# A trunk's squared-ReLU MLPs: two of the weight combinations of the seven-product scheme formed by adding DMAs, the down products reordered, one operand buffer moved

## The chip, the cores and the metric

The kernel runs on one core of a Trainium2 chip. The core has TensorE (PE) for matrix products, VectorE (DVE) and ScalarE (ACT) for elementwise work, GpSimd (POOL) and SyncE (SP), which here issues nearly all transfers. Each engine works off its own queue in program order and waits on semaphores for the others. The time is the device time of the one core, in microseconds (us).

## The reference, cut to what matters

Four layers, each a mixer (latent attention or gated linear attention) and then an MLP with a squared ReLU. There are two MLPs (here MLP 0 and MLP 1) with weights of their own, 512 tokens, D = 1024 and a hidden width of 4096:

```python
def rms_norm(x, gain):
    xf = x.astype(jnp.float32)
    y = xf * lax.rsqrt(jnp.mean(xf * xf, axis=-1, keepdims=True) + EPS)
    return (y * gain.astype(jnp.float32)).astype(x.dtype)

def sq_relu_mlp(xn, w_up, w_down):
    hid = jnp.square(jax.nn.relu(xn @ w_up))
    return hid @ w_down

x = x + mix.astype(x.dtype)
x = x + sq_relu_mlp(rms_norm(x, norm_mlp[i]), w_up, w_down)
```

All data is float32. The change touches the two MLPs alone.

## The kernel before

**Numbers in two parts.** A float32 operand is split into a high and a low part (`split`, line 108): ScalarE writes the high part `wh` (line 112), VectorE the rest `wl` (line 115). A product is three matmuls, high by high, high by low and low by high. `piece` (line 145) splits 128 x 1024 values of weights; three pairs of `wh` and `wl` exist.

**Seven products in place of eight.** The MLP's products are done in the scheme of Strassen and Winograd: tokens, the contracted dimension and the output are each halved, and of a weight block's quarters 11, 12, 21 and 22 and sums of them come seven products. In `up_block` (line 838 on) a block is 512 of the 4096 hidden columns; its quarters of 512 KB are called `a11`, `a12`, `a21` and `a22`, each in a tile `raw` (128 x 1024 values) out of five buffers. The steps are s1 (11), s2 (12), s5 (the sum `s`), s6 (`s` less `a11`), s3 (`a12` less that), s7 (`a11` less `a21`) and s4 (22). The sums of weights are formed by VectorE: line 904 `s = a21 + a22`, line 919 `s - a11`, line 925 `a12 - s`, line 932 `a11 - a21`. The activations stand in tiles x0 to x7 and in the combinations T1 to T4, made once for each MLP by `combine`; a tile T0 to T3 of the profile holds one 128 rows of all four. Line 818 is the matmul of both directions. A product of a block is one piece, 24 matmuls of 128 x 256.

**Outputs.** Products that share a part of their sum go on in one PSUM bank; `seed` copies a bank. s3 and s7 add a stored product to the bank (lines 928 and 935), `finish` scales by the norm's reciprocal root and cuts at zero (line 862) and ScalarE squares (line 863). In s7 the bank read by line 935 is the one to which s4 (T4) adds next, so s4 of the same block waits for that read.

**Order.** Blocks 0 and 1 run first (their first steps while the mixer still ends), one after the other; their second halves, `a21` and `a22`, come by two transfers of 1 MB in the buffers of the down weights (line 1116). From block 2 on, the down products of the pair before are put between the steps of the up blocks. `down_block` (line 944 on) takes two blocks of hidden columns: quarters of 1 MB in three buffers (line 950), seven products of two pieces each. There VectorE forms `S = 21 + 22` (line 987), `S - 11` (line 992), `11 - 21` (line 1004) and `12 - S` (line 1019). The moving operand is the split hidden tile `h` in two buffers, h0 and h1, used in turn (`operand`). The steps of the order within an engine come from a scheduler that sets each engine's queue.

**Loads.** All weights come by SP, line 852 for the up quarters and 950 for the down quarters. A load waits until the tile's buffer has been read by its former users, and in SP's queue for the loads ahead of it. POOL issues only two small loads, at the start of the kernel.

**Pads.** `PADS` holds bytes that are left free at the start of pools, to place the operands' addresses mod 512; `hidden` is that between h1 and h0 for MLP 0 and MLP 1.

Of the kernel before, what the change touches and what calls it, by code (L numbers as in the profile page):

```python
# [49 lines left out]
def trunk_kernel(ctx: ExitStack, tc: tile.TileContext, t_in: dict, out: bass.AP, out_row: bass.AP):  # L50
# [40 lines left out]
    PADS = dict(stage=224, right=64, up=320, masks=256, keep=128, hidden=(0, 0), down_w=(224, 224))  # L91
# [9 lines left out]
    pad(opened("edge", "right"), PADS["right"])  # L101
# [164 lines left out]
    class QuadNorm(Norm):  # L266
# [25 lines left out]
        def combine(self, k, t):  # L292
            g1, g2 = (gcol(self.g, self.g0 + j) for j in (k, k + KH))
            u, v = xT[k], xT[k + KH]
            t1, t2, t3, t4 = (t[:, i] for i in range(4))
            ACT.activation(t3, u[:, second], AF.Copy, scale=g1)
            DVE.scalar_tensor_tensor(t3, v[:, second], g2, t3, ALU.mult, ALU.subtract)
            DVE.scalar_tensor_tensor(t2, u[:, first], g1, t3, ALU.mult, ALU.add)
            DVE.scalar_tensor_tensor(t4, v[:, first], g2, t2, ALU.mult, ALU.subtract)
            DVE.scalar_tensor_tensor(t1, v[:, second], g2, t2, ALU.mult, ALU.subtract)  # L300
            return t

        def difference(self, k):
            DVE.tensor_tensor(xT[k][:, second], xT[k][:, second], xT[k + KH][:, second], ALU.subtract)
# [481 lines left out]
    def out_proj(w2d, X, nxt, after, begun=None):  # L786
        for c in range(4):
# [14 lines left out]
            if c < 3:  # L802
                nxt.pair(c)
                nxt.difference(c)


    def mlp(layer, nrm, nxt, final=False):
# [5 lines left out]
        def wide_raw():  # L813
            return pool_of("down_w").tile([P, 4, 512], F32, tag="raw", bufs=3, name=uname("raw"))
# [21 lines left out]
        Q, wide, turn = {}, {}, [0, 1]  # L836

        def up_block(b):
# [20 lines left out]
            def finish(c, half, tk):  # L859
                qs = q[tk is second][:, 2 * half : 2 * half + 2]  # L860
                r = nrm.rstd[:, tk].unsqueeze(1).to_broadcast([P, 2, TH])
                DVE.scalar_tensor_tensor(qs, c, 0.0, r, ALU.max, ALU.mult)  # L862
# [37 lines left out]
            def s5():  # L900
                s = v["s"] = up.tile([P, KH, 256], F32, tag="raw", bufs=5, name=uname("raw"))
                if "a12" not in v:
                    v["a12"] = unit(0, 1)
                DVE.tensor_tensor(s, v["a21"], v["a22"], ALU.add)  # L904
# [11 lines left out]
            def s6():  # L916
                if b == 1:
                    seed(v["p1"])
                DVE.tensor_tensor(v["s"], v["s"], v["a11"], ALU.subtract)
# [4 lines left out]
            def s3():  # L924
                DVE.tensor_tensor(v["a12"], v["a12"], v["s"], ALU.subtract)  # L925
# [5 lines left out]
            def s7():  # L931
                DVE.tensor_tensor(v["a21"], v["a11"], v["a21"], ALU.subtract)  # L932
# [11 lines left out]
        def down_block(s):  # L944
            last = s == NB // 2 - 2

            def quarter(dh, fh):
# [13 lines left out]
            def product(n, a, t, evac=None):  # L961
# [23 lines left out]
            def p5():
                v["21"], v["S"] = quarter(1, 0), quarter(1, 1)
                DVE.tensor_tensor(v["S"], v["21"], v["S"], ALU.add)
# [15 lines left out]
            def p7():  # L1003
                DVE.tensor_tensor(v["21"], v["11"], v["21"], ALU.subtract)
# [709 lines left out]
```

## Time and profile before

| | us |
|---|---|
| three runs | 1081.42, 1083.45, 1085.34 (median 1083.45) |
| the profiled execution's own time | 1080.79 |
| its span in the trace | 1079.1 |
| MLP 0, from the first block's T products to the last product | about 204 to 446 |
| MLP 1, the same | about 757 to 1002 |

The span runs from the first to the last instruction of the trace; the difference to the execution's own time (1.7 us) lies around it. The page's lines give busy time by engine and by group of instructions, the views of waits what released an engine that stood idle, and the windows the busy time of each engine in a stretch. A matmul's end is modelled, so the distance of two starts tells more of its price than its own duration (0.28 us for 128 x 256, started some 0.115 us apart).

### The profile page before, as it was taken

How to read it: one execution, taken by the hardware profiler on the slowest of the kernel's cores; microseconds unless marked ns; L12 is line 12 of the kernel's file. 1: busy time of each engine (PE TensorE's matmuls, PEld its weight loads, DVE VectorE, ACT ScalarE, POOL GpSimd, SP SyncE). 2: the span in 40 equal slices, each digit the busy share in tenths (PEclk: the TensorE clock that was granted, in tenths of full speed). 3: DMA queues.
4: the chain of work that ended last, by engine and by line, in shares of the span. 5: the costliest groups of instructions: out<-in, count | busy, mean ns of one | idle time of the engine just before them, and what ended most of it. 6: DMA issues, size and time to landing. Idle time of an engine off the chain costs nothing.

```text
span 1079.1 us, 17824 instructions
## 1 busy us (share of the span) xinstructions
PE 1058.9 (98%) x7322; PEld 977.1 (91%) x7322; DVE 890.0 (82%) x1210; ACT 640.2 (59%) x934; POOL 44.5 (4%) x78
## 2 busy tenths in 40 slices
PE   9999999989999999999999999999899999999997
PEld 7788888989999999988788888888899999999986
DVE  6789879999899899967565655678999899899865
ACT  6577655566667776644334735655565667766734
POOL 6400000000000000030000000000000000000000
PEclk9999999999999999999999999999999999999999
DMA  7312017143433433260222222234324423522412
GB/s 211 95 49 79 13 31 229 42 136 99 157 98 99 157 100 96 86 203 24 62 67 78 79 79 57 61 98 138 117 79 129 146 82 134 176 76 82 137 39 79
DMA packets 97969, 107.88 MB, mean 100 GB/s; under 512 B 8048, under 2 KB 72832, under 8 KB 97888
## 3 DMA queue, kind: packets, MB, share of 16 engines
q1 hardware_dynamic: 95872, 105.52, 31.1%
q8 instruction: 57, 0.93, 0.4%
q10 hardware_dynamic: 1952, 1.21, 0.4%
q0 software_dynamic: 64, 0.02, 0.1%
q14 instruction: 24, 0.20, 0.1%
HBM read 104.64 MB, written 2.10 MB: 99 GB/s over the span
## 4 chain that ended last, share of the span: by engine, by line
PE 84%; DVE 11%; issue 2%; ACT 2%; DMA 1%; SPq 0%; DVEq 0%; ACTq 0%
PE ps L818 39%; PE ps L120 12%; PE ps L122 12%; PE ps L121 12%; DVE wl L115 4%; PE ps L137 2%; PE ps L1371 2%; DMA wraw_ckv<-in_mla_w_in_dram 1%; DVE q L862 1%; DVE h L115 1%; DVE raw L925 1%; ACT wh L112 1%; DVE raw L932 1%; DVE raw L904 0%; PE ps L1408 0%
## 5 line engine op out<-in xcount | busy, mean ns | idle before, releaser
L112 ACT ACTIVATE wh<-raw 128x1024 fp32r<-128x1024 f32 x208 | 218.9, 1057 | 155.2 <-PE ps L818 84.3
L115 DVE TENSOR_TENSOR wl<-raw,wh 128x1024 fp32r<-128x1024 f32 x208 | 251.8, 1218 | 16.6 <-ACT wh L112 16.3
L818 PE MATMUL ps<-h,wh 128*128 128x256 f32 x1344 | 170.6, 279 | 0.0
L818 PEld LDWEIGHTS ps<-h,wh 128*128 128x128 f32 x1344 | 163.0, 188 | 0.0
L818 PE MATMUL ps<-h,wl 128*128 128x256 f32 x672 | 92.3, 279 | 2.1 <-DVE wl L115 2.1
L120 PE MATMUL ps<-set,wh 128*128 128x512 f32 x232 | 92.0, 397 | 0.7 <-ACT set L245 0.7
L121 PE MATMUL ps<-set,wh 128*128 128x512 f32 x232 | 91.2, 393 | 0.6 <-DVE set L246 0.6
L122 PE MATMUL ps<-set,wl 128*128 128x512 f32 x232 | 91.1, 393 | 0.0
L112 ACT ACTIVATE wh<-wraw 128x1024 fp32r<-128x1024 f32 x41 | 43.0, 1056 | 74.0 <-PE ps L122 41.5
L818 PEld LDWEIGHTS ps<-h,wl 128*128 128x128 f32 x672 | 84.5, 188 | 2.5 <-DVE wl L115 2.5
L863 ACT ACTIVATE q<-q 128x512 f32<-128x512 f32 x64 | 40.0, 629 | 46.4 <-DVE q L862 46.2
L120 PE MATMUL ps<-wh,set 128*128 128x512 f32 x144 | 59.7, 414 | 0.0
L115 DVE TENSOR_TENSOR wl<-wraw,wh 128x1024 fp32r<-128x1024 f32 x41 | 50.3, 1230 | 10.7 <-ACT wh L112 10.6
L115 DVE TENSOR_TENSOR h<-q,h 128x1024 fp32r<-128x1024 f32 x44 | 53.6, 1220 | 4.9 <-ACT h L112 4.9
L122 PE MATMUL ps<-wh,set 128*128 128x512 f32 x144 | 56.3, 391 | 0.0
L121 PE MATMUL ps<-wl,set 128*128 128x512 f32 x144 | 56.3, 391 | 0.0
L121 PEld LDWEIGHTS ps<-set,wh 128*128 128x128 f32 x232 | 44.0, 190 | 10.5 <-DVE set L246 1.3
L120 PEld LDWEIGHTS ps<-set,wh 128*128 128x128 f32 x232 | 43.9, 190 | 10.0 <-ACT set L245 1.0
L122 PEld LDWEIGHTS ps<-set,wl 128*128 128x128 f32 x232 | 44.0, 190 | 9.0
L112 ACT ACTIVATE h<-q 128x1024 fp32r<-128x1024 f32 x44 | 46.2, 1052 | 4.8 <-DVE q L988 2.1
L818 PE MATMUL ps<-T0h,wh 128*128 128x256 f32 x128 | 33.2, 283 | 7.1 <-DVE q L935 6.7
L120 PE MATMUL ps<-hh,wh 128*128 128x512 f32 x96 | 37.4, 389 | 0.0
(512 smaller groups left out, 2778.2 us busy)
## 6 DMA issues: line engine op xcount, KB each, us to landing
raw<-in_mlp_w_down_dram SPq DMA_DIRECT2D x38, 1024.0 KB, 5.2
raw<-in_mlp_w_up_dram SPq DMA_DIRECT2D x56, 512.0 KB, 3.9
wraw<-in_gla_w_in_dram SPq DMA_DIRECT2D x11, 1024.0 KB, 5.1
wraw<-in_mla_w_o_dram SPq DMA_DIRECT2D x8, 512.0 KB, 4.8
raw<-in_mlp_w_up_dram SPq DMA_DIRECT2D x4, 1024.0 KB, 8.0
wraw<-in_gla_w_o_dram SPq DMA_DIRECT2D x8, 512.0 KB, 4.9
xT<-in_x_dram SPq DMA_DIRECT2D x6, 256.0 KB, 7.5
wraw_qn<-in_mla_w_uq_dram SPq DMA_DIRECT2D x6, 256.0 KB, 3.4
```

The costliest lines, as they stand in the source:

```text
L112: raised.append(order(ACT.activation(hi, src, AF.Copy)))
L115: return lo_eng.tensor_tensor(lo, src, f(hi), ALU.subtract)
L120: PE.matmul(psum, wh, xh, start=start, stop=False, **kw)
L121: PE.matmul(psum, wh, xl, start=False, stop=False, **kw)
L122: PE.matmul(psum, wl, xh, start=False, stop=stop, **kw)
L137: PE.transpose(psum, src, ident[: src.shape[0], : src.shape[0]])
L818: return PE.matmul(p[:, m * TH : (m + 1) * TH], w[i][:, k - k0, m * P : (m + 1) * P], x[k][j], start=start, stop=stop, skip_group_check=True,)
L862: DVE.scalar_tensor_tensor(qs, c, 0.0, r, ALU.max, ALU.mult)
L863: ACT.activation(qs, qs, AF.Square)
L925: DVE.tensor_tensor(v["a12"], v["a12"], v["s"], ALU.subtract)
L932: DVE.tensor_tensor(v["a21"], v["a11"], v["a21"], ALU.subtract)
L1371: PE.matmul(p[:, t * 64 : (t + 1) * 64].rearrange("p (n c) -> p n c", c=m), k[:, sl], later, start=True, stop=True)
```

## The change

Two sums of the up weights and two of the down weights are no longer formed by VectorE. The one quarter is loaded by SP as before, and the other is added to it in SBUF by a second transfer, from POOL's queue, with `accum_op=ALU.add`, once the first has landed:

- `s = a21 + a22` (was line 904): a load of `a21` into the tile of `s` (new line 920) and an accumulate of `a22` (line 921). `a22` is still loaded for itself too.
- `a21 + a11` (was `a11 - a21`, line 932): `a21` is loaded as before (line 863), `a11` accumulated on it (line 865). For blocks 0 and 1 the transfers of 1 MB become two of 512 KB, one of them followed by an accumulate.
- the down block's `S = 22 + 21` (was line 987) and `21 + 11` (was line 1004): 1 MB each, loaded at line 973 and accumulated at 975.

An accumulate only adds. So subtractions turn into additions and other signs are turned round: the combinations of activations use the negated gains, `gains_less`, made once by one small instruction; a part of `finish` takes the minimum with zero where it took the maximum (the square is the same); part of the down sums is subtracted. Two elementwise additions of the down products' operands become instructions of three operands, of the same size.

Before, line 904 read the tiles that were loaded for themselves; now the accumulate waits for the plain load of `s`, and that load for a free buffer `raw`. The down products run in the order 1, 5, 6, 7, 4, 2, 3 (before 1, 5, 6, 7, 2, 3, 4), with quarters in the order S, 11, 21, 22, 12 in three buffers of their own names. The pads move h0, so that h1 and h0, which both lay at 288 mod 512 within a partition, lie at 288 and 192 in MLP 0 and at 288 and 448 in MLP 1. The other operands of the MLP's matmuls keep their places mod 512.

```diff
-    PADS = dict(stage=224, right=64, up=320, masks=256, keep=128, hidden=(0, 0), down_w=(224, 224))
+    PADS = dict(stage=224, up=320, masks=256, keep=128, hidden=(416, 160), down_w=(0, 64))
...
-    pad(opened("edge", "right"), PADS["right"])
+    less = opened("edge", "right").tile([P, 16], F32, name="gains_less")
...
+            l1, l2 = (less[:, self.g0 + j : self.g0 + j + 1] for j in (k, k + KH))
...
-            DVE.scalar_tensor_tensor(t2, u[:, first], g1, t3, ALU.mult, ALU.add)
-            DVE.scalar_tensor_tensor(t4, v[:, first], g2, t2, ALU.mult, ALU.subtract)
-            DVE.scalar_tensor_tensor(t1, v[:, second], g2, t2, ALU.mult, ALU.subtract)
+            DVE.scalar_tensor_tensor(t2, u[:, first], l1, t3, ALU.mult, ALU.subtract)
+            DVE.scalar_tensor_tensor(t4, v[:, first], l2, t2, ALU.mult, ALU.subtract)
+            DVE.scalar_tensor_tensor(t1, v[:, second], l2, t2, ALU.mult, ALU.subtract)
...
-        def difference(self, k):
-            DVE.tensor_tensor(xT[k][:, second], xT[k][:, second], xT[k + KH][:, second], ALU.subtract)
+        def total(self, k):
+            DVE.tensor_tensor(xT[k][:, second], xT[k][:, second], xT[k + KH][:, second], ALU.add)
...
+        ring = ["w0", "w2", "w1"]
+
+        def wide_raw(tag=None):
+            if tag is None:
+                tag = ring.pop(0)
+                ring.append(tag)
+            return pool_of("down_w").tile([P, 4, 512], F32, tag=tag, name=uname("raw"))
...
-                t = up.tile([P, KH, 256], F32, tag="raw", bufs=5, name=uname("raw"))
+                return fill(up.tile([P, KH, 256], F32, tag="raw", bufs=5, name=uname("raw")), half, trail)
+
+            def rows(half, trail):
                 c0 = b * FB + half * 256
-                with tc.issue_after(wide["last"].ins) if wide else nullcontext():
-                    SP.dma_start(t, w_up[trail * 512 : trail * 512 + 512, c0 : c0 + 256].rearrange("(k p) n -> p k n", p=P))
+                return w_up[trail * 512 : trail * 512 + 512, c0 : c0 + 256].rearrange("(k p) n -> p k n", p=P)
+
+            def fill(t, half, trail):
+                with tc.issue_after(wide["last"].ins) if "last" in wide and b > 1 else nullcontext():
+                    i = SP.dma_start(t, rows(half, trail))
+                if half and not trail:
+                    POOL.dma_start(t, rows(0, 0), accum_op=ALU.add)
+                if half and b < 2:
+                    wide["last"] = i
                 return t
+
+            fills.append(fill)
...
+                with tc.issue_after(wide["last"].ins):
+                    SP.dma_start(s, rows(1, 0))
+                POOL.dma_start(s, rows(1, 1), accum_op=ALU.add)
                 if "a12" not in v:
                     v["a12"] = unit(0, 1)
-                DVE.tensor_tensor(s, v["a21"], v["a22"], ALU.add)
...
-                DVE.tensor_tensor(v["s"], v["s"], v["a11"], ALU.subtract)
+                DVE.tensor_tensor(v["s"], v["s"], v["a11"], ALU.add)
...
-                DVE.tensor_tensor(v["a12"], v["a12"], v["s"], ALU.subtract)
+                DVE.tensor_tensor(v["a12"], v["a12"], v["s"], ALU.add)
...
-                DVE.tensor_tensor(v["a21"], v["a11"], v["a21"], ALU.subtract)
...
+            x, y, z = ring
+
+            def rows(dh, fh):
                 r0 = (2 * s + fh) * FB
-                SP.dma_start(t, w_dn[r0 : r0 + FB, dh * 512 : dh * 512 + 512].rearrange("(k p) n -> p k n", p=P))
+                return w_dn[r0 : r0 + FB, dh * 512 : dh * 512 + 512].rearrange("(k p) n -> p k n", p=P)
+
+            def quarter(tag, dh, fh, more=None):
+                t = wide_raw(tag)
+                SP.dma_start(t, rows(dh, fh))
+                if more:
+                    POOL.dma_start(t, rows(*more), accum_op=ALU.add)
                 return t
...
+                v["S"] = quarter(x, 1, 1, (1, 0))
+                v["11"] = quarter(y, 0, 0)
+                v["21"] = quarter(z, 1, 0, (0, 0))
                 product(1, v["11"], b11)
 
             def p5():
-                v["21"], v["S"] = quarter(1, 0), quarter(1, 1)
-                DVE.tensor_tensor(v["S"], v["21"], v["S"], ALU.add)
-                DVE.tensor_tensor(b11, b12, b11, ALU.subtract)
+                DVE.tensor_tensor(b11, b11, b12, ALU.subtract)
                 product(5, v["S"], b11)
 
             def p6():
-                DVE.tensor_tensor(v["S"], v["S"], v["11"], ALU.subtract)
-                DVE.tensor_tensor(b11, b22, b11, ALU.subtract)
+                DVE.tensor_tensor(v["S"], v["S"], v["11"], ALU.add)
+                DVE.scalar_tensor_tensor(b11, b11, -1.0, b22, ALU.mult, ALU.subtract)
 
                 def u2(p4):
                     DVE.tensor_tensor(acc[6], p4, acc[1], ALU.add)
...
                 product(6, v["S"], b11, u2 if last else None)
 
             def p7():
-                DVE.tensor_tensor(v["21"], v["11"], v["21"], ALU.subtract)
+                v["22"] = quarter(y, 1, 1)
                 DVE.tensor_tensor(b12, b22, b12, ALU.subtract)
 
                 def u3(p4):
...
 
                 product(7, v["21"], b12, u3 if last else None)
 
+            def p4():
+                v["12"] = quarter(z, 0, 1)
+                DVE.scalar_tensor_tensor(b11, b11, -1.0, b21, ALU.mult, ALU.subtract)
+                product(4, v["22"], b11)
+
             def p2():
-                v["12"] = quarter(0, 1)
                 product(2, v["12"], b21)
 
             def p3():
-                DVE.tensor_tensor(v["S"], v["12"], v["S"], ALU.subtract)
-                product(3, v["S"], b22)
-
-            def p4():
-                a = quarter(1, 1)
-                DVE.tensor_tensor(b21, b21, b11, ALU.subtract)
-                product(4, a, b21)
-
-            return [p1, p5, p6, p7, p2, p3, p4]
+                DVE.tensor_tensor(v["12"], v["12"], v["S"], ALU.add)
+                product(3, v["12"], b22)
+
+            ring[:] = [y, x, z]
+            return [p1, p5, p6, p7, p4, p2, p3]
...
-            t = wide[b] = wide_raw().rearrange("p a (b n) -> p (a b) n", b=2)
-            c0 = b * FB + 256
-            wide["last"] = SP.dma_start(t, w_up[:, c0 : c0 + 256].rearrange("(k p) n -> p k n", p=P))
+            t = wide[b] = wide_raw(f"w{b}").rearrange("p a (b n) -> p (a b) n", b=2)
+            for trail in (0, 1):
+                fills[b](t[:, trail * KH : trail * KH + KH], 1, trail)
```

The order on VectorE at the start of MLP 0, before: block 1's `s` (raw_2548) is made by line 904 out of raw_2250, which has `a21` and `a22` of block 1, ahead of three splits; line 935 is the read of block 0's bank q_2253.

```order
L904 TENSOR_TENSOR raw_2548<-raw_2250 128x1024
L115 TENSOR_TENSOR wl_2456<-raw_2146,wh_2455 128x1024
L115 TENSOR_TENSOR wl_2488<-raw_2248,wh_2487 128x1024
L932 TENSOR_TENSOR raw_2250<-raw_2156,raw_2250 128x1024
L928 TENSOR_TENSOR q_2253<-ps_2392,mt_2452 128x512
L115 TENSOR_TENSOR wl_2519<-raw_2248,wh_2518 128x1024
L862 SCALAR_TENSOR_TENSOR q_2253<-q_2253,rstd_2327 128x512
L115 TENSOR_TENSOR wl_2552<-raw_2548,wh_2551 128x1024
L935 TENSOR_TENSOR q_2253<-ps_2279,mt_2421 128x512
```

The same place now: `s` of block 0 is raw_2394, `s` of block 1 raw_2552, both written by transfers.

```order
L115 TENSOR_TENSOR wl_2399<-raw_2394,wh_2398 128x1024
L115 TENSOR_TENSOR T3l_2327<-q_2314,T3h_2326 128x1024
L938 TENSOR_TENSOR raw_2394<-raw_2394,raw_2145 128x1024
```

```order
L115 TENSOR_TENSOR wl_2523<-raw_2248,wh_2522 128x1024
L947 TENSOR_TENSOR q_2257<-ps_2397,mt_2457 128x512
L115 TENSOR_TENSOR wl_2557<-raw_2552,wh_2556 128x1024
L879 SCALAR_TENSOR_TENSOR q_2257<-q_2257,rstd_2331 128x512
L938 TENSOR_TENSOR raw_2552<-raw_2552,raw_2157 128x1024
L953 TENSOR_TENSOR q_2257<-ps_2283,mt_2426 128x512
L944 TENSOR_TENSOR raw_2159<-raw_2159,raw_2552 128x1024
```

Lines 904 and 932 are gone. The split `wl` of block 0's `s` now stands ahead of T3l, and the read of block 0's bank (line 935, now 953) stands behind the split of block 1's `s` and behind the next use of `s`, line 938 (was 919).

On POOL's queue, where no load of weights stood in either MLP, the accumulates of MLP 0 begin so (line 865 `a21 + a11`, 921 `s`, 975 the down weights):

```order
L865 DMA raw_2248<-in_mlp_w_up_dram 128x4x256
L865 DMA raw_2252<-in_mlp_w_up_dram 128x4x256
L921 DMA raw_2394<-in_mlp_w_up_dram 128x4x256
L921 DMA raw_2552<-in_mlp_w_up_dram 128x4x256
L865 DMA raw_2716<-in_mlp_w_up_dram 128x4x256
L975 DMA raw_2788<-in_mlp_w_down_dram 128x4x512
L921 DMA raw_2752<-in_mlp_w_up_dram 128x4x256
```

On SP's queue the two loads of `s` stand behind the quarters `a11` and `a12` of blocks 0 and 1 (raw_2145 to raw_2159) and ahead of block 2's (raw_2714 on):

```order
L863 DMA raw_2157<-in_mlp_w_up_dram 128x4x256
L863 DMA raw_2159<-in_mlp_w_up_dram 128x4x256
L920 DMA raw_2394<-in_mlp_w_up_dram 128x4x256
L920 DMA raw_2552<-in_mlp_w_up_dram 128x4x256
L863 DMA raw_2714<-in_mlp_w_up_dram 128x4x256
```

Before, these two rows were not there; the load of raw_2552 waits for the buffer of raw_2145, whose last reader is line 938 of block 0 above.

More of the change, by code (lines that the diff above doesn't have):

```diff
@@ L803, in out_proj @@
                 nxt.pair(c)
-                nxt.difference(c)
+                nxt.total(c)
     def mlp(layer, nrm, nxt, final=False):
@@ L811, in mlp @@
         up = pool_of("up")
-        def wide_raw():
-            return pool_of("down_w").tile([P, 4, 512], F32, tag="raw", bufs=3, name=uname("raw"))
+        ring = ["w0", "w2", "w1"]
[4 more added lines that the diff above has]
+            return pool_of("down_w").tile([P, 4, 512], F32, tag=tag, name=uname("raw"))
         def matmuls(p, w, k0, ks, ms, x, begin, end):
@@ L834, in matmuls @@
                 one(1, 0, k, m, False, end and k == 3)
-        Q, wide, turn = {}, {}, [0, 1]
+        Q, wide, turn, fills = {}, {}, [0, 1], []
         def up_block(b):
@@ L861, in finish @@
                 r = nrm.rstd[:, tk].unsqueeze(1).to_broadcast([P, 2, TH])
-                DVE.scalar_tensor_tensor(qs, c, 0.0, r, ALU.max, ALU.mult)
+                DVE.scalar_tensor_tensor(qs, c, 0.0, r, ALU.min if half else ALU.max, ALU.mult)
                 ACT.activation(qs, qs, AF.Square)
@@ L945, in down_block @@
             last = s == NB // 2 - 2
-            def quarter(dh, fh):
-                t = wide_raw()
+            x, y, z = ring
+            def rows(dh, fh):
                 r0 = (2 * s + fh) * FB
-                SP.dma_start(t, w_dn[r0 : r0 + FB, dh * 512 : dh * 512 + 512].rearrange("(k p) n -> p k n", p=P))
+                return w_dn[r0 : r0 + FB, dh * 512 : dh * 512 + 512].rearrange("(k p) n -> p k n", p=P)
[4 more added lines that the diff above has]
+                    POOL.dma_start(t, rows(*more), accum_op=ALU.add)
                 return t
@@ L973, in product @@
                 elif begin and n in (2, 3, 4, 5):
-                    DVE.tensor_tensor(acc[n], p4, acc[n], ALU.add)
+                    DVE.tensor_tensor(acc[n], p4, acc[n], ALU.add if n < 4 else ALU.subtract)
                 else:
@@ L1052, in down @@
                         a_type(p, w, hid, cols=slice(j * P, (j + 1) * P))
-                        DVE.tensor_tensor(xT[m], p, xT[m], ALU.add)
+                        DVE.tensor_tensor(xT[m], p, xT[m], ALU.subtract if b < NB - 1 and m >= KH else ALU.add)
                         if b == NB - 1:
@@ L1126, in mlp @@
         nrm.finish()
-        nrm.difference(KH - 1)
+        nrm.total(KH - 1)
         for b in range(2):
@@ L1550, in trunk_kernel @@
     turns = rope_turns()
+    DVE.tensor_scalar(less, gains[:, GAIN_COL["mlp"] : GAIN_COL["mlp"] + 16], -1.0, None, ALU.mult)
     O, begun = mla(0, nrm, w0, mla_pools)
```

1 line of the change is left out of this document (removed).

## The prediction

> **What bounds the kernel now.** I read the page first: the busy row and the chain that ended last.
>
> ```profile
> PE 1058.9 (98%) x7322; PEld 977.1 (91%) x7322; DVE 890.0 (82%) x1210; ACT 640.2 (59%) x934; POOL 44.5 (4%) x78
> PE 84%; DVE 11%; issue 2%; ACT 2%; DMA 1%; SPq 0%; DVEq 0%; ACTq 0%
> PE ps L818 39%; PE ps L120 12%; PE ps L122 12%; PE ps L121 12%; DVE wl L115 4%; PE ps L137 2%; PE ps L1371 2%; DMA wraw_ckv<-in_mla_w_in_dram 1%; DVE q L862 1%; DVE h L115 1%; DVE raw L925 1%; ACT wh L112 1%; DVE raw L932 1%; DVE raw L904 0%; PE ps L1408 0%
> ```
>
> TensorE is busy 98% of the span. VectorE, from which the change takes work, is 82% busy and on 11% of the chain. So what counts is the few places where TensorE stands still. The view of TensorE's waits names those of the MLP's products (L818); its columns are the releaser, the total, the times and the longest:
>
> ```profile
> PE ps L818 <- DVE q L935: 6.7, 4, 2.0
> PE ps L818 <- DVE wl L115: 2.4, 3, 1.1
> PE ps L818 <- ACT wh L112: 1.4, 3, 0.5
> ```
>
> The windows show where they lie (PE, PEld, DVE, ACT, POOL busy, clock, DMA share, GB/s; MLP 0 first, then MLP 1):
>
> ```profile
> 204.00:210.00 6.00, 5.53 (x47) 5.33 (x46) 6.00 (x7) 4.37 (x6) 0.00 (x0) 1.00 0.07 13
> 210.00:220.00 10.00, 8.23 (x71) 8.05 (x70) 10.00 (x12) 4.95 (x8) 0.00 (x0) 1.00 0.71 215
> 220.00:233.00 13.00, 11.47 (x98) 11.11 (x98) 12.93 (x14) 9.59 (x12) 0.00 (x0) 1.00 0.47 155
> 233.00:432.00 199.00, 199.00 (x1731) 199.00 (x1730) 188.54 (x169) 132.74 (x151) 0.00 (x0) 1.00 0.35 112
> 432.00:446.00 14.00, 12.93 (x112) 12.73 (x111) 14.00 (x14) 8.23 (x11) 0.00 (x0) 1.00 0.24 77
> ```
>
> ```profile
> 754.00:770.00 16.00, 13.54 (x113) 12.94 (x112) 16.00 (x18) 7.60 (x10) 0.00 (x0) 1.00 0.27 73
> 770.00:788.00 18.00, 16.21 (x126) 16.05 (x127) 16.88 (x18) 11.53 (x14) 0.00 (x0) 0.91 0.51 170
> 987.00:1002.00 15.00, 13.94 (x121) 13.74 (x120) 15.00 (x15) 9.23 (x12) 0.00 (x0) 1.00 0.21 71
> ```
>
> TensorE's idle time is window minus busy: 0.47 + 1.77 + 1.53 = 3.8 us where MLP 0 starts, 2.46 + 1.79 = 4.3 us where MLP 1 starts, 1.07 and 1.06 us at their ends. In between (233 to 432) it has no gap at all although VectorE is 95% busy: less VectorE work there is worth nothing. In all, some 10 us can be won from VectorE's relief, and all of it lies in four places.
>
> **What goes from VectorE.**
>
> ```profile
> L904 DVE TENSOR_TENSOR raw<-raw,raw 128x1024 f32<-128x1024 f32 x12 | 14.6, 1219 | 0.1
> L904 DVE TENSOR_TENSOR raw<-raw 128x1024 f32<-128x1024 f32 x4 | 4.9, 1219 | 0.0
> L932 DVE TENSOR_TENSOR raw<-raw,raw 128x1024 f32<-128x1024 f32 x16 | 19.5, 1219 | 0.1
> L987 DVE TENSOR_TENSOR raw<-raw,raw 128x2048 f32<-128x2048 f32 x6 | 13.7, 2286 | 1.3 <-DMA raw<-in_mlp_w_down_dram 1.2
> L1004 DVE TENSOR_TENSOR raw<-raw,raw 128x2048 f32<-128x2048 f32 x6 | 13.7, 2283 | 0.0
> ```
>
> 32 x 1.22 + 12 x 2.28 = 66 us of VectorE work disappear. The other sign changes keep their size, and the new `gains_less` is one small instruction.
>
> **What is added.** 44 accumulating transfers from POOL's queue, 32 of 512 KB and 12 of 1 MB, and 16 plain loads of 512 KB for `s`. Nothing of the accumulating kind runs now; the nearest rows (KB each, median us from issue to landing):
>
> ```profile
> raw<-in_mlp_w_up_dram SPq DMA_DIRECT2D x56, 512.0 KB, 3.9
> tmp<-in_gla_w_gk_up_dram ACTq DMA_DIRECT2D x6, 32.0 KB, 1.8
> pos_i<-in_positions_dram POOLq DMA_DIRECT2D x1, 2.0 KB, 4.5
> invf<-in_inv_freq_dram POOLq DMA_DIRECT2D x1, 16.0 KB, 6.9
> ```
>
> Call L the time from the plain load's landing to the accumulate's landing, for 512 KB. Floor: as quick as SP's load, 3.9. The size itself is worth 3.9 - 1.8 = 2.1 us, so POOL's 4.5 becomes 6.6 and its 6.9 becomes 9.0. POOL's two rows stem from the crowded first microseconds, so I take **L = 6**, nearer to 6.6 than to the floor, and keep 3.9 to 9.0. [...]
>
> **The start of MLP 0, where L counts twice.** The rows that time it:
>
> ```profile
> 186.90 1.22 DVE L115 TENSOR_TENSOR T2l<-raw,T2h 128x1024 fp32r<-128x1024 f32 x1
> 203.41 1.22 DVE L919 TENSOR_TENSOR raw<-raw,raw 128x1024 f32<-128x1024 f32 x1
> 217.02 0.36 PE L818 MATMUL ps<-T0h,wh 128*128 128x256 f32 x1 [1.77 <-DVE q L935]
> 235.50 0.28 PE L818 MATMUL ps<-x0h,wh 128*128 128x256 f32 x1
> L112 ACT ACTIVATE wh<-raw 128x1024 fp32r<-128x1024 f32 x208 | 218.9, 1057 | 155.2 <-PE ps L818 84.3
> ```
>
> Before, L904 made block 1's `s` within VectorE's queue, 1.22 us after its turn came. Now the load of `s` needs a buffer of `raw`, and there are five. Block 0's takes the one that T2l frees at 186.9 + 1.2 = 188.1: issue and landing 0.4 + 3.9 give 192.4, the accumulate 192.4 + L. Behind it stand ScalarE's wh (1.06) and, in VectorE's order, wl, T3l and L938, each about 1.14 from start to start and the last 1.22: 192.4 + L + 1.06 + 3.5 = 197.0 + L. Only L938 of block 0, the last reader of `a11`, frees the buffer for block 1's `s`. That lands, loaded and accumulated, at 197.0 + L + 4.3 + L = 201.3 + 2L. Then wh 1.06, wl 1.14, the scaling L879 0.6, L938 1.14 and L953 0.68 follow on VectorE, and L953 (block 0's last-but-one output, L935 before) is what block 0's T4 on TensorE waits for: with some 0.1 us of hand-over **T4 starts at 206.0 + 2L**, 218.0 for L = 6, against 217.02. What waits behind wl in VectorE's queue is all that TensorE needs next. From T4 to block 2's first product are six pieces of 2.76 us (24 matmuls at 0.115) and the 0.8 us that a wait like L935's keeps: 17.4 us, before 235.50 - 217.02 = 18.5. So block 2 starts at 223.4 + 2L: gain 12.1 - 2L, which is +0.1 for L = 6. The cap is 2.6 us: without the waits of 1.77 and 0.47 the pieces ahead still end at 214.8, L953 follows them, and 17.4 us later it is 232.9.
>
> **The start of MLP 1, where L counts once.**
>
> ```profile
> 756.18 0.69 DVE L221 SCALAR_TENSOR_TENSOR rstd<-mt,mt 128x512 f32<-128x512 f32 x1
> 770.39 0.36 PE L818 MATMUL ps<-T0h,wh 128*128 128x256 f32 x1 [1.97 <-DVE q L935]
> 790.10 0.28 PE L818 MATMUL ps<-x0h,wh 128*128 128x256 f32 x1
> ```
>
> Here too T2l frees the buffer for block 0's `s`, but ScalarE splits `s` only behind the root and the squares, so that this first accumulate is there in time for L up to about 10. L904, L932 and a wl that stood ahead of the root L221 in VectorE's queue are gone or behind it, so it can end near 754.0 in place of 756.9 (not earlier: ScalarE hands its input over at 752.1). But the split of `s` now stands behind two scalings (0.6 each), the last square (0.6) and wh (1.06): wl at 756.9, L938 done at 759.2. Load 4.3, L, and the same 4.9 us chain: T4 at 768.4 + L, block 2 at 785.8 + L against 790.10. Gain 4.3 - L, that is **-1.7 for L = 6**.
>
> **The ends.** At 432 and 987 VectorE is busy all the time and TensorE idles 1.07 and 1.06 us. L932 of the last block goes there: I take 1.5 of 2.1 us.
>
> **The addresses.** The down products read their moving tile `h` from two buffers, both at 288 mod 512 in the program before; T tiles lie at 192 and the weights wh at 0. Starts of matmuls of one piece:
>
> ```profile
> 206.42 0.28 PE L818 MATMUL ps<-T1h,wh 128*128 128x256 f32 x1
> 207.67 0.28 PE L818 MATMUL ps<-T3l,wh 128*128 128x256 f32 x1
> 279.76 1.91 PE L818 MATMUL ps<-h,wh 128*128 128x256 f32 x15
> 281.51 1.09 PE L818 MATMUL ps<-h,wl 128*128 128x256 f32 x8
> ```
>
> T: 1.25 us for 11 steps, 0.1136. h: 1.75 for 15, 0.1167. One of the two buffers moves, 480 matmuls of each MLP. In MLP 0 it moves to 192, where T lies: 480 x 3.1 ns = **1.5 us gained**. In MLP 1 it moves to 448, where no MLP matmul of this trace reads; T gives the best case, -1.5, and the opposite, as much again, +1.5. I take 0.
>
> **Middle of the MLP.** A block's `s` is loaded once the block before has split its T3 operand, seven pieces, 19 us, ahead of need; 4.3 + L and the splits take some 13. No wait up to L of about 10. The stretch moves 112 GB/s of loads now at a DMA share of 0.35, so the accumulates have room.
>
> **Sum against the profiled execution** (1080.79 us; span 1079.1): starts -0.1 and +1.7, ends -1.5, addresses -1.5 and 0: -1.4 us, 1079.4. The median of the runs, 1083.45, is 2.7 above that execution; I forecast on it: 1083.45 - 1.4 = **1082.0**. A measurement here tells about 0.3% (3.2 us) from no change, so this is "the same, leaning faster".
>
> **Rivals.**
> - *The accumulate is as quick as a load, L below 5.4.* At L = 4 the starts give 2.6 + 0.3; with the ends and addresses -5.9: 1077.5. For it: queues are nearly empty at 200 to 204. Against: POOL's rows.
> - *The accumulate is slow, L from 7.5 up: slower than before.* It decides at block 1's `s`: there the three terms of L cost 3 us for each us of L, with nothing beside it on TensorE. L = 9 gives +10.6 - 3.0, 1091. For it: 6.9 us for 16 KB; and the stretch 210 to 220 already moves 215 GB/s at a share of 0.71, to which the new transfers come.
> [...]
> - *Nothing but the addresses moves*, if the starts' gaps are kept by another wait: 1083.45 - 1.5, 1082. This lies in my forecast's band.
>
> **How the numbers follow.** Forecast (within 0.3%): 0.40, its own range 1080 to 1086.7. Quick accumulate, faster: 0.38. Slow accumulate 0.15 and held-back descriptors 0.07, slower: 0.22. The best case is L = 3.9, 2.6 and 0.4 at the starts, 2.1 at the ends, 3.0 by addresses: 1075.3; the runs of before lie 2 us to either side of their median, so I go to 1074. The slow end beyond L = 8.3 is left out, with about one case in ten: 1089.
>
> **What would show it.** DMA issues: POOL's row of 512 KB from `in_mlp_w_up_dram`, its landing is L. TensorE's waits: L953 at the two starts, or wh L112 with the accumulate behind it. The T4 after block 0's T3 at 206.0 + 2L and 768.4 + L. The pitch of h in each MLP, alternating pieces. No idle time between 233 and 432; if there is any, the loads of the middle are late and my view of that stretch is wrong. If T4 starts on time and the span still grows, the loss is one that I haven't named.

## The result, and the profile after

The changed kernel took **1113.27 us** (median of 4 runs, 1109.30 to 1114.31) beside 1083.63 before (1081.42 to 1085.34): ratio 1.0268, 95% interval 1.0236 to 1.0300. It is 30 us slower, far outside the range of 1074 to 1089.

The page of the changed kernel: busy time, the chain, and the DMA queues (q1 is that of SP, q0 that of POOL; packets, MB, share of 16 engines).

```profile
PE 1066.1 (96%) x7322; PEld 982.1 (88%) x7322; DVE 832.7 (75%) x1167; ACT 637.9 (57%) x934; POOL 99.7 (9%) x122
PE 55%; DVE 12%; DMA 10%; issue 3%; ACT 2%; ACTq 0%; DVEq 0%; POOLq 0%
...
q1 hardware_dynamic: 104384, 113.91, 32.4%
q0 software_dynamic: 23296, 29.38, 16.8%
```

VectorE lost 57 us of busy time (66 by the sum of single durations, as counted; instructions that follow each other closely overlap in the record: before, a split of 1.23 us starts at 197.06 and the next instruction at 198.21), and the span grew from 1079.1 to 1111.1. TensorE's idle time (span minus busy) grew by 24.8 us, from 20.2 to 45.0, and its busy time by 7.2 with the same 7322 matmuls. The chain has 10% of DMA where it had 1%. POOL's queue moved 29.38 MB in 16.8% of the engines' time, SP's 113.91 MB in 32.4%: an accumulated MB took 0.57% of the engines' time, one of SP's 0.28%.

TensorE's waits, ScalarE's largest one, and the DMA issues (KB each, us to landing):

```profile
PE ps L824 <- DVE q L953: 15.8, 4, 8.1
PE ps L824 <- ACT wh L112: 9.0, 8, 2.4
PE ps L824 <- ACT ps L992: 6.3, 2, 3.2
```

```profile
ACT wh L112 <- DMA raw<-in_mlp_w_up_dram: 71.8, 15, 8.0
```

```profile
raw<-in_mlp_w_up_dram SPq DMA_DIRECT2D x80, 512.0 KB, 5.9
raw<-in_mlp_w_down_dram SPq DMA_DIRECT2D x38, 1024.0 KB, 6.1
raw<-in_mlp_w_up_dram POOLq DMA_DIRECT2D x32, 512.0 KB, 7.5
raw<-in_mlp_w_down_dram POOLq DMA_DIRECT2D x12, 1024.0 KB, 10.2
```

L935's successor L953 costs 15.8 us in place of 6.7. ScalarE stood 71.8 us in 15 waits for the accumulates of `s` (line 921). SP's own 512 KB loads landed after 5.9 us, before 3.9.

Where the time went, by the start of the n-th of TensorE's matmuls of the MLP in both traces (line 818 before, 824 after; their number is the same):

| stretch | loss, us | how read |
|---|---|---|
| up to MLP 0 | 0.7 | matmul 0: 190.96, now 191.67 |
| start of MLP 0 | 7.6 | matmul 384: 240.94, now 249.27 |
| middle of MLP 0 | 2.9 | matmul 2016: 428.96, now 440.23 |
| end of MLP 0 | 4.1 | matmul 2351: 469.01, now 484.42 |
| start of MLP 1 | 8.8 | matmul 2736: 795.54, now 819.74 |
| middle of MLP 1 | 2.5 | matmul 4368: 984.52, now 1011.20 |
| end of MLP 1 | 5.4 | matmul 4703: 1024.52, now 1056.56 |

**The starts.** The timeline of MLP 0 (start, duration, engine, line, idle before and its releaser): the two accumulates of `s`, the splits that wait for them, L938 and T4.

```profile
193.01 1.28 POOL L921 DMA_DIRECT2D raw<-in_mlp_w_up_dram  x1 [33.61 <-DMA raw<-in_mlp_w_up_dram]
208.24 1.27 POOL L921 DMA_DIRECT2D raw<-in_mlp_w_up_dram  x1 [13.95 <-DVE rstd L221]
...
199.25 1.06 ACT L112 ACTIVATE wh<-raw 128x1024 fp32r<-128x1024 f32 x1 [4.07 <-DMA raw<-in_mlp_w_up_dram]
218.80 1.06 ACT L112 ACTIVATE wh<-raw 128x1024 fp32r<-128x1024 f32 x1 [5.97 <-DMA raw<-in_mlp_w_up_dram]
...
202.62 1.22 DVE L938 TENSOR_TENSOR raw<-raw,raw 128x1024 f32<-128x1024 f32 x1
...
223.50 0.58 PE L824 MATMUL ps<-T0h,wh 128*128 128x256 f32 x1 [6.14 <-DVE q L953]
```

Block 0's accumulate took 199.25 - 193.01 = 6.2 us, as estimated. Block 1's, started once the load behind L938 had landed, took 218.80 - 208.24 = **10.6 us**. In MLP 1 the same pair reads 780.57 and 789.53, 9.0 us, and T4 waits 8.06. Counted as the prediction counts L, from the landing of the plain load to that of the accumulate, the three are 6.7, 11.0 and 9.4 us. In MLP 1 TensorE waits 2.39 us more, ahead of block 0's T1 (773.75), and not for an accumulate: this one had landed by 770.13, but ScalarE takes up the split of `s` at 772.66 only, behind two squares.

**The clock.** Windows around that wait (PE, PEld, DVE, ACT, POOL busy, clock, DMA share, GB/s):

```profile
217.30:223.50 6.20, 0.07 (x1) 0.00 (x0) 3.61 (x5) 2.22 (x3) 2.55 (x2) 0.66 0.76 171
223.50:230.00 6.50, 6.50 (x32) 6.50 (x33) 3.79 (x5) 2.46 (x4) 0.00 (x0) 0.54 1.12 212
230.00:233.00 3.00, 3.00 (x29) 3.00 (x28) 1.96 (x2) 3.00 (x5) 0.00 (x0) 1.00 1.08 333
```

After the wait TensorE ran at a granted clock of 0.54: 32 matmuls in 6.5 us, then 29 in 3.0. 27 of them started 0.213 us apart in place of 0.114: 2.6 us on top of the wait. The same follows the 8.06 us (0.54 from 794.2 to 800.0) and the waits at the ends (0.57 from 458 to 462, 0.50 from 1029 to 1035). Before, one wait of 1.97 us, at 768.4, had this effect (0.72 from 770 to 776).

**The ends.** Product 4 now follows product 7, whose last VectorE sum (L1035) makes what ScalarE copies into product 4's bank (L992):

```profile
440.21 1.23 DVE L115 TENSOR_TENSOR wl<-raw,wh 128x1024 fp32r<-128x1024 f32 x1 [5.11 <-ACT wh L112]
...
455.69 1.22 DVE L1035 TENSOR_TENSOR xT<-xT,sum 128x1024 f32<-128x1024 f32 x1
```

```profile
458.02 3.62 PE L824 MATMUL ps<-h,wh 128*128 128x256 f32 x16 [3.17 <-ACT ps L992]
```

VectorE stood 5.11 us behind a split that waited for an accumulate, then worked without a gap and was late with L1035.

### The profile page after: what moved, and what is told of

Its sections match the earlier page's. It is cut to its first block, busy times and chain, and to the rows that moved or that the text cites. A ratio compares the mean times of both kernels' runs of the same rounds, so it can differ in the third digit from the quotient of the medians.

```text
span 1111.1 us, 17962 instructions
## 1 busy us (share of the span) xinstructions
PE 1066.1 (96%) x7322; PEld 982.1 (88%) x7322; DVE 832.7 (75%) x1167; ACT 637.9 (57%) x934; POOL 99.7 (9%) x122
## 3 DMA queue, kind: packets, MB, share of 16 engines
q1 hardware_dynamic: 104384, 113.91, 32.4%
q0 software_dynamic: 23296, 29.38, 16.8%
## 4 chain that ended last, share of the span: by engine, by line
PE 55%; DVE 12%; DMA 10%; issue 3%; ACT 2%; ACTq 0%; DVEq 0%; POOLq 0%
PE ps L824 26%; DMA raw<-in_mlp_w_up_dram 10%; PE ps L120 8%; PE ps L122 8%; PE ps L121 8%; DVE wl L115 5%; PE ps L1396 2%; ACT wh L112 2%; DVE h L115 1%; DVE raw L1017 1%; DVE raw L938 1%; DVE q L879 1%; DMA raw<-in_mlp_w_down_dram 1%; PE ps L1433 0%; PE ps L137 0%
## 5 line engine op out<-in xcount | busy, mean ns | idle before, releaser
L112 ACT ACTIVATE wh<-raw 128x1024 fp32r<-128x1024 f32 x208 | 218.3, 1055 | 179.3 <-DMA raw<-in_mlp_w_up_dram 71.8
L865 POOL DMA_DIRECT2D raw<-in_mlp_w_up_dram x16 | 20.7, 1292 | 494.5 <-DMA raw<-in_mlp_w_up_dram 347.6
L115 DVE TENSOR_TENSOR h<-q,h 128x1024 fp32r<-128x1024 f32 x44 | 53.6, 1221 | 10.1 <-ACT h L112 10.1
L824 PE MATMUL ps<-T0h,wh 128*128 128x256 f32 x128 | 34.7, 293 | 23.4 <-DVE q L953 15.8
## 6 DMA issues: line engine op xcount, KB each, us to landing
raw<-in_mlp_w_down_dram POOLq DMA_DIRECT2D x12, 1024.0 KB, 10.2
```

What stands on the lines that cost most here:

```text
L112: raised.append(order(ACT.activation(hi, src, AF.Copy)))
L115: return lo_eng.tensor_tensor(lo, src, f(hi), ALU.subtract)
L824: return PE.matmul(p[:, m * TH : (m + 1) * TH], w[i][:, k - k0, m * P : (m + 1) * P], x[k][j], start=start, stop=stop, skip_group_check=True,)
L865: POOL.dma_start(t, rows(0, 0), accum_op=ALU.add)
```

## The experiments

All ratios are to the kernel before, run on the same chip. Gains on the changed kernel, in us, are differences of medians to 1113.27. That median had 1083.63 of before beside it, those of the experiments 1081.67 to 1082.05, so by the ratios a gain is some 2 us smaller.

**1. The order of the down products (e1_order).**

```diff
-                v["12"] = quarter(z, 0, 1)
+                if not last:
+                    v["12"] = quarter(z, 0, 1)
...
+                if last:
+                    v["12"] = quarter(z, 0, 1)
...
-            return [p1, p5, p6, p7, p4, p2, p3]
+            return [p1, p5, p6, p7, p2, p3, p4] if last else [p1, p5, p6, p7, p4, p2, p3]
```

> The changed kernel, but the last down block of each MLP in the old order 1, 5, 6, 7, 2, 3, 4 (quarter 12 loaded ahead of product 2). Theory A (order): the waits of 3.17 us at 454.85 and 1025.82 come from product 4 standing right behind product 7, whose three VectorE sums (L1033 to L1035) write acc[4] before ScalarE may seed product 4's bank; with the clock at half behind them they cost 3.7 and 4.9 us by the marks of TensorE's program. It expects both waits gone and 1113 - 8.5 = 1105 us. Rival B (the accumulates' transfers are late there too): the waits stay, 1113.

Measured 1108.67, ratio 1.0242 (1.0228 to 1.0256): 4.6 us less, not 8.5; by the ratios it is 2.8, and the intervals of the two kernels overlap. Both waits for L992 are gone, and by TensorE's matmuls the two ends are 5.1 and 6.2 us shorter than in the change. But the middles lose 1.9 us more each (a wait of 1.35 us at 359.8 became 2.02 at 361.7 and one of 0.74 at 930 became 2.33 at 928.7, both behind accumulates of `s`), and 2.0 and 2.2 us come back right behind the two MLPs' last matmul of line 824. The order takes part, and the rest did not stay as it was.

**2. Blocks 0 and 1 without accumulates (e2_start).**

```diff
-                if half and not trail:
+                if half and not trail and b > 1:
                     POOL.dma_start(t, rows(0, 0), accum_op=ALU.add)
...
-                with tc.issue_after(wide["last"].ins):
-                    SP.dma_start(s, rows(1, 0))
-                POOL.dma_start(s, rows(1, 1), accum_op=ALU.add)
+                if b > 1:
+                    with tc.issue_after(wide["last"].ins):
+                        SP.dma_start(s, rows(1, 0))
+                    POOL.dma_start(s, rows(1, 1), accum_op=ALU.add)
...
+                if b < 2:
+                    DVE.tensor_tensor(s, v["a21"], v["a22"], ALU.add)
...
+                if b < 2:
+                    DVE.tensor_tensor(v["a21"], v["a11"], v["a21"], ALU.add)
```

> The changed kernel, but blocks 0 and 1 of each MLP form s and a21 + a11 on VectorE again, without accumulates; all later blocks keep theirs. Theory A (chain of load and accumulate behind block 0's s6, L = 9 to 10.5 us in the crowd of SP's loads): the waits of 6.14 and 8.06 us go, and with them the half clock behind: 8.4 and 9 us less, 1096. Rival B (the accumulates load the DMA engines and slow everything a little): less than 5 us, 1108 or more, since 36 of 44 accumulates stay.

Measured 1103.14, ratio 1.0190 (1.0174 to 1.0205): 10.1 us less, between the two. The waits of 6.14 and 8.06 us became 1.85 and 1.96. By TensorE's matmuls the loss up to matmul 384 is 1.3 us in place of 8.3, and the start of MLP 1 (matmul 2352 to 2736) adds 1.6 in place of 8.8. The middle, though, loses more than it did: 8.1 us between matmuls 384 and 2208 of MLP 0 (from 1.3 to 9.4), where the change lost 7.3.

**3. The pads alone (e3_pads)**, on the kernel before.

```diff
-    PADS = dict(stage=224, right=64, up=320, masks=256, keep=128, hidden=(0, 0), down_w=(224, 224))
+    PADS = dict(stage=224, right=64, up=320, masks=256, keep=128, hidden=(416, 160), down_w=(320, 64))
```

> The kernel before with the pads alone, so that h0 lies at 192 (MLP 0) and 448 (MLP 1) mod 512, other operands where they were. Theory: the pitch of h from the moved buffer falls from 116.8 to 113.5 ns in both MLPs, 480 matmuls each, 3.2 us: 1080.4, ratio 0.997. Rival (the pitch saved is lost at the next wait, since VectorE is 95% busy): 0.999 to 1.000.

Measured 1081.19, ratio 0.9988 (0.9979 to 0.9996): 0.9 us. TensorE's busy time fell by 2.7 us and its idle time rose. Between the matmuls 480 and 2112 of each MLP the pitch gives 1.4 and 1.0 us. At the ends a part of it is lost again: the waits for wl of 1.07 and 1.06 us became 1.62 each, since TensorE comes earlier to the same split. The largest loss, 2.9 us, lies at the start of MLP 0, ahead of the first matmul that reads `h` (the MLP's matmul 384), so the pitch cannot be its cause. Two waits for L935 are longer there, 1.85 us at 216.53 in place of 1.77 and this one:

```profile
234.09 0.38 PE L818 MATMUL ps<-T0h,wh 128*128 128x256 f32 x1 [2.04 <-DVE q L935]
```

The windows behind them have a clock of 0.66 (216.5 to 220) and 0.72 (234 to 240). Before, the second wait had 1.53 us and the clock stayed at 1.00; in MLP 1 it is the other way round, the half clock of before (0.72 from 770 to 776) does not come here (1.00 from 772 to 778). Why the waits differ by these tenths stays open.

**4. Plain loads in place of the accumulates (e4_plain).** It leaves out the additions of the second quarters.

```diff
-                    POOL.dma_start(t, rows(0, 0), accum_op=ALU.add)
+                    POOL.dma_start(t, rows(0, 0))
```

(and the same at the two other places)

> The changed kernel with every accumulate of POOL's queue replaced by a plain load of the same bytes to the same place, waits unchanged; it leaves out the addition of the second quarter to the first. If the read-modify-write is the price, the landing of POOL's 512 KB falls from 7.5 us to near SP's 4 to 5, that of 1 MB from 10.2 to 6 or 7, the queue's share of the engines from 16.8% to 8 or 9%, and the time by 8 us or more. [...]

Measured 1083.05 in a single run, beside 1082.05 before. POOL's rows and queue in its page:

```profile
q0 software_dynamic: 7936, 29.38, 8.5%
...
raw<-in_mlp_w_up_dram POOLq DMA_DIRECT2D x32, 512.0 KB, 4.8
raw<-in_mlp_w_down_dram POOLq DMA_DIRECT2D x12, 1024.0 KB, 6.0
```

ScalarE's waits for up weights:

```profile
ACT wh L112 <- DMA raw<-in_mlp_w_up_dram: 27.3, 8, 5.8
```

The same bytes, issued by the same engine after the same waits, land in 4.8 and 6.0 us in place of 7.5 and 10.2, at half the share. So the price is that of accumulating, not of POOL's queue as such; and 2.7 us a transfer in landing, with twice the share, make about 30 us of the span. What in it costs is not separated: POOL's queue has 23296 packets in the changed kernel, where an accumulate of 512 KB is 512 packets of 1024 B, and 7936 here for the same bytes, and POOL spent 1.28 us on issuing an accumulate of `s` in place of 0.75 on the plain load.

The second transfer behind the first is not free when it is plain. In MLP 1 block 0's T1 waits 2.39 us here too (757.39), T4 then 5.26 (775.07), and the start of MLP 1 loses 6.0 us by TensorE's matmuls. The rest of the MLPs makes up for it: 0.8 us at the start of MLP 0, 1.4 and 2.4 in the middles, 1.1 and 0.4 at the ends.

**5. Edits 1 and 2 together (e5_both).**

> Both edits: the last down block in the old order and blocks 0 and 1 without accumulates. If their costs are independent, the measured gains add: 1113.3 - 10.1 - 4.6 = 1098.5. If the order only costs where VectorE is behind its time because of a late accumulate, the sum differs: up to 3.2 + 3.2 us of wait and as much of half clock go at the two ends, 1094. What is then left above 1082 are late accumulates of the middle: 12 us or more.

Measured 1095.55, ratio 1.0129 (1.0112 to 1.0147): 17.7 us less, where the single gains add to 14.7. By the ratios it is 15.1 against 11.2, and the intervals of the four kernels together leave some 4.5 us open, so that the two parts are not independent is not shown by this. ScalarE still waits 54.4 us for up weights; 13.7 us are left above before.

**6. Room for `s` of blocks 0 and 1 (e6_early).**

```diff
-                s = v["s"] = up.tile([P, KH, 256], F32, tag="raw", bufs=5, name=uname("raw"))
+                s = v["s"] = acc[6 + b] if b < 2 else up.tile([P, KH, 256], F32, tag="raw", bufs=5, name=uname("raw"))
```

> The changed kernel, but s of blocks 0 and 1 stands in the tiles sum6 and sum7, which nothing uses before the first down block; so both loads of s issue at once and neither waits for block 0's s6. Accumulates as in the change. Chain theory: the waits of 6.14 and 8.06 us before T4 go although the accumulates stay: 8 us less in each MLP at least, 1097, near or below e2_start. Contention theory (the accumulate itself is late in the crowd, wherever it starts): the waits stay above 3 us each, 1107 or more.

Measured 1098.99, ratio 1.0155 (1.0132 to 1.0178): 14.3 us less (12.2 by the ratios) with all 44 accumulates kept, and those of `s` in blocks 0 and 1 still landing 6.3 to 9.9 us after their issue. ScalarE's waits for the two tiles:

```profile
ACT wh L112 <- DMA sum<-in_mlp_w_up_dram: 2.6, 2, 1.7
```

T4 of block 0 waits 1.60 and 1.50 us in place of 6.14 and 8.06. At the starts it was the chain: the buffer freed by L938, then the load, then the accumulate. Late accumulates of later blocks remain (56.6 us of ScalarE's waits).

**7. No accumulate of `s` anywhere (e7_no_s).**

```diff
-                POOL.dma_start(s, rows(1, 1), accum_op=ALU.add)
...
+                DVE.tensor_tensor(s, v["a21"], v["a22"], ALU.add)
+                DVE.tensor_tensor(v["a11"], s, v["a11"], ALU.subtract)
...
-                product(v["x5"], s, "T1", True)
+                product(v["x5"], v["a11"], "T1", True)
...
-                DVE.tensor_tensor(v["s"], v["s"], v["a11"], ALU.add)
```

> The changed kernel without the second load of a21 and without the accumulate of s: t = (a21 + a11) + a22 on VectorE is T2's operand, and a11 := t - a11 in place T1's. The accumulates of a21 + a11 and those of the down weights stay (28 of 44). Theory: only the accumulates of s are waited for (ScalarE's splits stood 71.8 us for them, for the others nobody), so all waits ended by a DMA go: 1083 to 1088. Rival: the accumulate on a21 is now needed at T1, three products earlier than at T3, and takes the place of s: waits of wh ended by a DMA stay, 1100.

Measured 1080.83, ratio 0.9990 (0.9979 to 1.0001). Of the 30 us nothing is left, with 28 accumulates still there and the new order of the down products too: its wait for L992 is 0.3 us at each end. ScalarE's waits for up weights:

```profile
ACT wh L112 <- DMA raw<-in_mlp_w_up_dram: 1.7, 1, 1.7
```

The rival is true once: block 2's accumulate is late at its new place (VectorE waits 2.37 us for it at 222.5, TensorE then 4.46 before T4 at 233.59).

**8. A version from the parts that help (e8_best).** `a21 + a11` is accumulated in blocks 0 and 1 alone, where it is issued 17 to 44 us ahead of the sum that reads it; T1's and T2's operands there as in e7_no_s; later up blocks by VectorE; down accumulates and pads of the change; old order in the last down block.

> A version meant to be faster than both: a21 + a11 by accumulate only in blocks 0 and 1, loaded some 40 us ahead of need; there t and t - a11 by VectorE as in e7_no_s, one VectorE sum less per block than before. Later up blocks by VectorE as before, down sums by accumulates, the last down block in the old order, the pads of the change. Theory: no wait ended by a DMA, at each start 2.4 us of VectorE less where TensorE idles 3.8 and 4.3, the pads' 3 us of pitch kept because the down sums are off VectorE: 1082 - 3 - 3 = 1076, ratio 0.994. Rival: the down accumulates slow the loads and the gain is lost in the middle: 1082 or more.

Measured 1076.76, ratio **0.9952** (0.9940 to 0.9965), as expected: faster than both.

Four variants of it, each with one part undone or moved:

> e8_best with the pads of before (h0 and h1 both at 288). Theory: alone (e3_pads) the pads gave 0.9 us of their 3.2, because the ends, where VectorE is the bound, took the rest; with the down sums off VectorE they should be worth more, so that without them the time is 1076.8 + 2 to 3 = 1079 to 1080. Rival: they are worth 0.9 here too, 1077.7.

e9_nopads: 1083.58, ratio 1.0014 (1.0003 to 1.0025). More than either theory had. POOL's accumulates for blocks 0 and 1 start at 191.31 and 748.25 here and at 155.39 and 734.23 in e8_best: SP's loads ahead of them are issued at 186.90 in place of 150.73, as I read it because with other pads the wide tiles lie over other former tiles and wait for other readers. So the difference of the two times is not the pitch's. The marks show the pitch by itself: from matmul 480 to 2112 of each MLP e8_best gains 1.6 us on e9_nopads.

> e8_best with the down sums 22 + 21 and 21 + 11 on VectorE again (12 operations of 2.28 us), so that four accumulates are left, two at each start. Theory: the down accumulates are in time and free VectorE at the ends and at block 2, where TensorE waits; without them 1 to 3 us are lost, 1078 to 1080. Rival (they crowd the loads as much as they relieve VectorE): 1076 or less.

e10_nodown: 1079.10, ratio 0.9974 (0.9960 to 0.9988): 2.3 us more than e8_best by the medians, with intervals that overlap. The traces do not put that on the down products: the MLPs, each from its first matmul of line 824 to its last, are 1.5 and 1.6 us shorter than in e8_best, whose T4 of block 1 is followed by the half clock (0.72 from 232 to 238), and 3.2 and 1.7 us are lost right behind the two MLPs (a wait of 1.02 us for ScalarE at 466.27 is one part). So that the down accumulates gain anything is not shown.

> e8_best with the order 1, 5, 6, 7, 4, 2, 3 in the last down block too. Theory: the order costs only where VectorE is behind because of a late accumulate; here the wait for L992 is 0.3 us at each end, as in e7_no_s, and the time 1077.5. Rival (the order costs 3 us at each end by itself, clock included): 1081 or more.

e11_neworder: 1076.44, ratio 0.9950 (0.9936 to 0.9964): the order as such costs nothing that this can tell.

> e8_best with pads of 512 bytes in place of 416 and 160, so that h0 lies at 288 mod 512 again while the wide tiles of MLP 0 keep a place whose former readers end early (in e9_nopads the accumulates of blocks 0 and 1 came 36 us later in MLP 0, since the wide tiles overlapped other tiles). Theory: 960 matmuls at 3.3 ns, 3.2 us more than e8_best or e11_neworder, 1079.5 to 1080; in MLP 0 the pitch of h alone differs, 1.6 us by TensorE's marks. Rival: all of the 6.8 us between e8_best and e9_nopads belong to the pitch, 1083.

```diff
-    PADS = dict(stage=224, up=320, masks=256, keep=128, hidden=(416, 160), down_w=(0, 64))
+    PADS = dict(stage=224, up=320, masks=256, keep=128, hidden=(512, 512), down_w=(0, 64))
```

e12_h288: **1074.69**, ratio 0.9939 (0.9925 to 0.9952), the lowest median of all, against both theories, though its interval overlaps those of e8_best and e11_neworder. The pitch was as expected: from matmul 480 to 2112, e8_best gains 1.6 us on it in each MLP. But up to matmul 384, where no matmul reads `h` yet, e8_best loses 1.5 us in MLP 0 and 4.2 in MLP 1 on it. A part of that is the clock behind longer waits before T4 of block 1. First e8_best, then e12_h288: T4 of block 1, and the window from there on.

```profile
232.08 0.56 PE L824 MATMUL ps<-T0h,wh 128*128 128x256 f32 x1 [2.04 <-DVE q L956]
```

```profile
232.00:238.00 6.00, 5.92 (x37) 5.92 (x38) 5.29 (x7) 2.23 (x3) 1.27 (x1) 0.72 0.62 93
```

```profile
231.61 0.39 PE L824 MATMUL ps<-T0h,wh 128*128 128x256 f32 x1 [1.62 <-DVE q L956]
```

```profile
231.50:237.50 6.00, 5.89 (x51) 5.89 (x52) 6.00 (x8) 2.88 (x4) 1.27 (x1) 1.00 0.57 90
```

37 matmuls in 6 us against 51. The wait is 0.42 us longer, and the half clock behind it takes 1.4 us more; in MLP 1 the same comes again (0.72 from 785 to 791, against 1.00). VectorE has the same work there, only some tenths later against TensorE; why is open, and the variants that differ by 2 us do not rank the pads.

## Why the prediction was wrong, step by step

- **The step that failed is "L = 6", one figure for every accumulate.** It held for the one that ran nearly alone (6.2 from its issue). Block 1's, on which all depended, had 10.6 and 9.0: SP's next loads are issued beside it (207.33, 209.07 and 213.62 in MLP 0), and the accumulates took 16.8% of the engines' time where plain loads of the same 29.38 MB took 8.5% (experiment 4). The packet records of all 32 accumulates of 512 KB in the changed kernel bear this out: while other queues moved at most 1.0 MB during their flight, they landed after 6.0 to 8.3 us, beside 1.5 to 2.5 MB after 8.9 to 11.0. I had kept 9.0 as the upper end, and given "slow, from 7.5 up" 0.15: that rival came true, and the side with it.
- **L alone does not make the loss.** With 6.7, 11.0 and 9.4 in the prediction's own formulas the time is 1091, still 22 us short. From the forecast of -1.4 to the 32.0 of the traces, 14.8 us were missed at the starts, 11.0 at the ends and 6.9 in the middles (0.7 lie ahead of MLP 0); the next points say where they come from.
- **The chain of the starts was right.** 206.0 + 6.7 + 11.0 = 223.7 for T4; measured 223.50. In MLP 1 the formula's 768.4 (its chain is taken as 4.9 us where MLP 0's adds up to 4.7), moved by the 15.4 us lost before, gives 793.2 with 9.4; measured 794.23. There it leaves out the late split that costs T1 of block 0 its 2.39 us. Experiment 6 took the wait for the buffer away and the waits went.
- **What a wait costs was too low.** I counted only the wait. Behind 6.14, 8.06 and twice 3.17 us the clock was halved (0.54, 0.54, 0.57 and 0.50 in the windows behind them): 2.6, 2.3, 1.7 and 2.7 us by the spacing of the matmuls, 9.3 in all against 1.6 before. These 7.7 us more, less the 2.7 that the pads took in experiment 3, are most of the 7.2 us by which the busy time grew; the other 2 were not traced.
- **"No wait up to L of about 10" in the middle was wrong.** I took 4.3 us for the load of `s` and 19 us of time. In the trace the load is issued behind a 1 MB load, takes 8.0, the accumulate 7.6, and ScalarE waits for them:

```profile
344.42 0.37 SPq L920 DMA_DIRECT2D raw<-in_mlp_w_up_dram  x1
...
352.39 1.30 POOL L921 DMA_DIRECT2D raw<-in_mlp_w_up_dram  x1 [12.07 <-DVE q L879]
...
360.00 1.06 ACT L112 ACTIVATE wh<-raw 128x1024 fp32r<-128x1024 f32 x1 [6.98 <-DMA raw<-in_mlp_w_up_dram]
```

15.6 us from issue to split, and they were due some 14 after the issue: TensorE waits 1.35 us for the piece at 361.11. With plain loads (4.8) TensorE has no wait over 0.8 us left in the middles, nor without accumulates of `s`.
- **The ends, "-1.5", came out at +4.1 and +5.4.** The order of the down products, which I had not priced at all, puts L1035 ahead of product 4. It cost 3.17 us and a halved clock (0.57 and 0.50) where VectorE was behind because of a late accumulate, and 0.3 us where it was not (e7_no_s, e11_neworder).
- **The addresses** did what they should at 192, and at 448, where I took 0, the same: h from the moved buffer starts 113.3 ns apart in both MLPs, from the other 116.8, 480 matmuls of each MLP moved. But 3.2 us of pitch gave 0.9 us of time (e3_pads): 1.1 us were lost where TensorE came earlier to the same split at the ends, and more to half clock at the start of MLP 0 (0.66 and 0.72 behind its two waits), which the pitch does not touch.
- **The held-back descriptors**, with a chance of 0.07 (POOL's transfers delayed by VectorE's work), were a guess of mine, and no run shows such a delay: in experiment 4 POOL issued as many transfers of the same bytes beside the same VectorE work, and they landed in 4.8 us (512 KB). In the changed kernel itself the packets of the accumulate of 193.01 moved from 195.0 to 198.8 while VectorE was busy nearly without a break (to 197.7), and POOL's issue of an accumulate of `s` took 1.27 to 1.30 us every time.

## What to carry to other kernels

Before an addition is moved from an engine to an accumulating transfer, ask whether the operand is loaded long before it is needed: here a version that accumulates only sums issued 17 to 44 us ahead, and down weights, is 5 us faster than before (e8_best, the pads and one VectorE sum less included), and with the sums loaded just in time the kernel lost 30. Count the added transfer as a second latency behind the first, at the landing times of the crowded stretch and not of the quiet one (11.0 us against 6.7 here), with the engine share that was measured for it (here 16.8% against 8.5% for the same bytes loaded). A shorter matmul pitch gained nothing ahead of a wait that it only lengthened (1.07 us became 1.62 in e3_pads), and a wait cost more than its length (6.14 us, and 2.6 more at half clock behind it).

## What the runs showed of the hardware that was not expected

- **An accumulating load of float32** from POOL's queue landed after 7.5 us (512 KB) and 10.2 us (1 MB) by the medians of the changed kernel, a plain one from the same queue after 4.8 and 6.0 (e4_plain). For the same 29.38 MB the queue had 23296 packets in place of 7936, and 16.8% of the DMA engines' time in place of 8.5%. POOL spent 1.28 us on issuing an accumulate of `s`, 0.75 on the plain load in its place.
- **The granted clock was halved around some of TensorE's waits.** In the windows behind them it was 0.54 (6.14 and 8.06 us), 0.57 and 0.50 (3.17 us each) in the changed kernel, 0.72 behind 1.97 us before, 0.66 and 0.72 behind 1.85 and 2.04 us in e3_pads, and 0.72 behind 2.04 us in e8_best. It stayed at 1.00 behind 1.77 and 1.53 us before (217 to 220 and 232 to 240) and behind 1.62 us in e12_h288. The length alone didn't decide in these runs: 1.85 us did it in e3_pads (0.66 from 216.5 to 220) and not in e2_start (1.00 from 218 to 222). What else decides was not shown.
- **How long it was halved.** Inside the MLPs the clock stood at 0.50 for 10.24 us (219.30 to 229.54 and 789.33 to 799.57), 3.41 (458.23 to 461.65) and 6.83 (1028.26 to 1035.09) in the changed kernel, and for 3.41 (771.19 to 774.60) before. Behind 6.14 and 8.06 us it set in while TensorE still waited: T4 starts at 223.50 and 794.23.
